# Changed places of weight splits, query products and a first up step in a two-layer encoder

## The chip, the cores and the metric

The program runs on one core of a Trainium2 chip. The metric is the device time of one launch in microseconds (us). The engines are TensorE (PE in the profile; its weight loads are PEld), VectorE (DVE), ScalarE (ACT), GpSimd (POOL) and SyncE (SP, which here only issues DMAs). "Granted clock" is the share of TensorE's full rate (2.4 GHz) that the trace records: 1.00 is the upper level, 0.50 the lower one (1.2 GHz).

## What is computed

A trunk of two layers on x of 1024 positions by 1024 channels, float32. Layer 0 mixes with an mLSTM, layer 1 with attention in a window of 128 positions to either side; both are followed by a SwiGLU with D_FF = 2816.

```python
def swiglu(h, w_in, w_out):
    gu = h @ w_in
    gate, up = gu[..., :D_FF], gu[..., D_FF:]
    return (jax.nn.silu(gate) * up) @ w_out

def window_attn_mixer(h, positions, w_in, sink, w_out):   # 16 query heads, 4 key heads, head 64, block L = 128
    proj = h @ w_in
    ...
    q = rope(q, positions).reshape(B, NB, L, Hkv, G, hd)
    k = rope(k, positions)
    ...                                                   # a block sees its own 128 keys and the 128 on either side
    scores = jnp.einsum('bcqhgd,bckhd->bchgqk', q, k_band) * (hd ** -0.5)
    scores = jnp.where(mask[None, :, None, None], scores, -jnp.inf)
    m = jnp.maximum(jnp.max(scores, axis=-1), sink_l)
    p = jnp.exp(scores - m[..., None])
    denom = jnp.sum(p, axis=-1) + jnp.exp(sink_l - m)
    out = jnp.einsum('bchgqk,bckhd->bcqhgd', p, v_band) / denom...
    return out.reshape(B, S, Hq * hd) @ w_out

def reference(...):
    for i in range(2):
        hn = rmsnorm(x, norm_mix_w[i])
        x = x + (mlstm_mixer if i == 0 else window_attn_mixer)(hn, ...)
        x = x + swiglu(rmsnorm(x, norm_ffn_w[i]), ffn_w_in[i], ffn_w_out[i])
    return rmsnorm(x, norm_final_w)
```

## The kernel before

x is held transposed, 8 rows of 128 channels by 1024 positions. A product of two float32 matrices is three products of parts: every operand is cut into a high part (ACT: L187 for weights, L200 or L204 for values) and what is left of it (POOL: L188 for weights; DVE: L201 or L205 for values), and the multiplications are high by high, high by low and low by high. wh and wl are the two parts of a weight tile, hh and hl those of a row of hidden values, raw and hraw what a DMA brought in. Weight tiles come by `ahead()`, which splits the next tile and starts the load of one further on; `w()` takes the tile that was split. Each engine works off its own list of instructions in the order in which the program issues them, and waits only for the operands and buffers of the next one. That order is the source's; where two kinds of work are mixed, `weave(main, fill)` spreads the pieces of the second list between those of the first.

The up half of a feed-forward (`ffn_up`, L535) has 22 steps f, one for each 128 hidden channels. It uses a scheme of seven half products for a two-by-two split of the weights and of the channels, with sums of weights and sums of channel rows as operands: `left()` makes the weight side of a step (wa, wb, wc, wd with a trailing h or l), and `self.forms` holds the channel side, four pairs of rows (f, f12, f23, f34). Each call of `seven` (L525) is one half product over the four pairs k, 12 matmuls of 512 columns at L530, into one PSUM bank; `pa`, `pe`, `pb`, `pc`, `pd` are the banks, and pa and pb take a second product on top. DVE, ACT and POOL then form silu(gate) times up (L551 to L584) with R, the reciprocal root of the norm, and the step's row goes to HBM (`hkeep`, L586). Between the products `more()` issues one item of `todo`, mostly the split of the next step's weights; in the last step it issues `hidden` (L589), which brings a row back and cuts it into hh and hl.

The down half (`ffn_down`) works in chunks of rows; the first chunk has six. Before it begins it issues the rest of the `hidden` calls, one `ahead()` for the first weight tile and `load_x`. For each d of eight output rows and each half of the positions it issues 18 matmuls at L616 and adds the bank to x (L643); in the first half of each d it calls `ahead()` for the weights of the next one, and behind each d `hidden` for a row of the next chunk.

The attention (`attn`, L1341) first computes keys and the queries of group 0 (`rope_in`), then the values (L476). Queries and keys with their rotation go to HBM (`bounce`, L1175) and come back in the shape that the scores need (`load_q` L1211, `load_k` L1219), which takes a round trip. Then a loop of 35 rounds i runs over 32 units (4 groups of heads by 8 blocks) in a pipeline: round i issues the scores and the softmax of unit i (`attn_soft`: matmul L1259, mask and maximum L1264 on DVE, exponential L1268 and L1269 on ACT, sums L1274 and L1275 on DVE, scaling L1276 on POOL), the transposes of unit i-2 (L1288) and the product with the values of unit i-3 (L1303, results to `ykeep` L1317 for groups 0 and 1). A unit of eight at position 6 of its group also issues the loads of the next group's queries and keys. Between these pieces stand the query products of groups 1 to 3: `qs` has 144 parts of two matmuls each (L228), twelve parts make one product, and four products one group, whose finished values go through `bounce`. They are spread evenly over the rounds 0 to 19:

```python
if i < NQ:                        # NQ = 20
    k = len(qs) * (i + 1) // NQ
    fill, nq = qs[nq:k], k
```

From round 20 on the output products of groups 0 and 1 (`outs`, also L228) fill the rounds; `take_back` (L699) brings the stored results of a group back from `ykeep` in round 19 and 20 and cuts them. Behind the loop `out_pair(self.y23, True)` adds the other two groups; behind every second row of it `norm_forms` makes the channel side of the next up half and squares the rows into the norm sum (R, L292; matmuls of the norm sum L364), and at its last quarter (`i == 3`) it issues `left()`, all weight sides of the first up step.

## Time and profile before

| | |
|---|---|
| time, median of 3 runs | 2365.91 us (2365.62 to 2366.03) |
| profiled execution, its own time | 2360.96 us |
| its span, first to last instruction | 2359.2 us |
| mean granted clock of TensorE | 0.978 |
| chain that ended last | PE 80%, DVE 6%, DMA 4%, issue 4%, POOL 3%, ACT 2% |
| three longest lines of that chain | L530 36% (up), L616 21% (down), L228 12% (dense and output products) |

The profiled execution is one of its own, 4.95 us below the median of the timed runs, and 1.76 us of it lie outside the span. All start times below count from the span's beginning. On this span layer 0's up half ends near 959 us, its down half near 1190; the attention's loop lies between 1300 and 1590, layer 1's up half between 1642 and 2085. A line of a timeline reads: start, duration, engine, line, operation, output <- inputs, shape, count, and in square brackets how long the engine had been idle before it and what released it.

### The profile page before, as it was taken

Reading aid. Unit: us, or ns where it says so; the run is one execution under the profiler, and the core shown is the slowest. Engines: PE = TensorE matmul, PEld = TensorE weight load, DVE = VectorE, ACT = ScalarE, POOL = GpSimd, SP = SyncE. Lnnn points to the kernel's source line nnn. Section 1 sums busy time; section 2 is a strip of 40 time slices with the busy share of each in tenths; the row PEclk is TensorE's granted clock in tenths of the full one; section 3 lists DMA queues with packets and bytes.
Section 4 is the critical chain, followed back from the end, with each engine's and each line's share of the span. In section 5 each row is a group of like instructions: output and inputs, shape, how many; then the busy total and the mean of one; then the engine's idle time right before and its main releaser. Section 6 shows DMA issues by size and latency. Waiting matters only on the chain.

```text
span 2359.2 us, 28227 instructions
## 1 busy us (share of the span) xinstructions
PE 2225.9 (94%) x10655; PEld 1827.1 (77%) x10655; DVE 1409.1 (60%) x2603; ACT 834.3 (35%) x1533; POOL 602.3 (26%) x410
## 2 busy tenths in 40 slices
PE   6999999989999999899998888798999999989998
PEld 3889988867888888688877766586788888868887
DVE  6455656688666666671233767778866666643113
ACT  3334445353222222221322666674322222232021
POOL 4212213311111111230432444550111111123043
PEclk9999999999999999999999999999999999999999
DMA  3111114132222222541315134602222222264112
GB/s 120 50 36 46 63 37 152 54 116 72 81 81 81 81 83 87 214 134 45 107 54 169 52 117 126 217 10 98 90 81 81 81 81 81 76 222 131 45 54 72
DMA packets 75960, 216.76 MB, mean 92 GB/s; under 512 B 8320, under 2 KB 14976, under 8 KB 75824
## 3 DMA queue, kind: packets, MB, share of 16 engines
q1 hardware_dynamic: 64216, 177.07, 23.1%
q10 hardware_dynamic: 11608, 37.89, 4.0%
q8 instruction: 84, 1.38, 0.2%
q14 instruction: 52, 0.43, 0.1%
HBM read 159.15 MB, written 55.77 MB: 91 GB/s over the span
## 4 chain that ended last, share of the span: by engine, by line
PE 80%; DVE 6%; DMA 4%; issue 4%; POOL 3%; ACT 2%; SPq 1%; POOLq 0%; ACTq 0%; DVEq 0%
PE mm L530 36%; PE mm L616 21%; PE mm L228 12%; PE mm L476 4%; PE pn L212 2%; DMA slab<-bounce 1%; DMA bounce<-slab 1%; PE sc L1259 1%; PE mx L1303 1%; PE tp L1288 1%; POOL wl L188 1%; PE pk L212 1%; DMA slab<-ykeep 1%; POOL e L1276 1%; DVE hnl L205 0%
## 5 line engine op out<-in xcount | busy, mean ns | idle before, releaser
L188 POOL TENSOR_TENSOR wl<-raw,wh 128x1024 fp32r<-128x1024 f32 (+2 forms) x96 | 231.0, 2410 | 593.2 <-ACT wh L187 372.2
L616 PE MATMUL mm<-hh,wh 128*128 128x512 f32 (+1 forms) x768 | 290.8, 379 | 13.1 <-ACT wh L187 13.1
L616 PE MATMUL mm<-hh,wl 128*128 128x512 f32 (+1 forms) x768 | 290.1, 378 | 3.1 <-POOL wl L188 3.1
L616 PE MATMUL mm<-hl,wh 128*128 128x512 f32 (+1 forms) x768 | 290.3, 378 | 0.0
L568 POOL TENSOR_TENSOR t<-t,R 128x512 f32<-128x512 f32 x44 | 57.5, 1308 | 618.1 <-ACT t L567 618.1
L616 PEld LDWEIGHTS mm<-hh,wh 128*128 128x128 f32 x768 | 145.6, 190 | 42.5 <-ACT wh L187 14.0
L643 DVE TENSOR_TENSOR x<-x,mm 128x512 f32<-128x512 f32 x80 | 54.9, 686 | 202.6 <-PE mm L616 202.6
L616 PEld LDWEIGHTS mm<-hh,wl 128*128 128x128 f32 x768 | 145.6, 190 | 33.0 <-POOL wl L188 4.5
L616 PEld LDWEIGHTS mm<-hl,wh 128*128 128x128 f32 x768 | 145.7, 190 | 28.6
L228 PE MATMUL mm<-slab,wh 128*128 128x512 f32 x512 | 153.0, 408 | 8.4 <-ACT wh L187 5.1
L567 ACT ACTIVATE t<-t 128x512 f32<-128x512 f32 x44 | 27.8, 632 | 329.0 <-DVE t L566 328.9
L530 PE MATMUL mm<-f12h,wbh 128*128 128x512 f32 x352 | 138.8, 395 | 0.4 <-ACT wbh L200 0.4
L530 PE MATMUL mm<-f12h,wbl 128*128 128x512 f32 x352 | 138.8, 394 | 0.0
L530 PE MATMUL mm<-f12l,wbh 128*128 128x512 f32 x352 | 138.6, 394 | 0.0
L187 ACT ACTIVATE wh<-raw 128x1024 fp32r<-128x1024 f32 (+3 forms) x106 | 102.0, 969 | 72.5 <-DVE hl L201 56.6
L228 PE MATMUL mm<-hnh,wh 128*128 128x512 f32 x416 | 126.4, 404 | 0.9 <-DVE x L643 0.9
L228 PE MATMUL mm<-hnh,wl 128*128 128x512 f32 x416 | 124.7, 400 | 0.0
L228 PE MATMUL mm<-hnl,wh 128*128 128x512 f32 x416 | 124.1, 399 | 0.0
L560 DVE TENSOR_TENSOR t<-mm,t 128x512 f32<-128x512 f32 x44 | 30.4, 692 | 154.3 <-PE mm L530 154.3
L228 PEld LDWEIGHTS mm<-slab,wh 128*128 128x128 f32 x512 | 96.4, 193 | 29.1 <-ACT wh L187 6.3
L1276 POOL TENSOR_TENSOR e<-e,smd 128x768 f32<-128x768 f32 (+1 forms) x64 | 87.4, 1369 | 121.9 <-DVE smd L1275 69.2
L530 PE MATMUL mm<-f34h,wd 128*128 128x512 f32 x352 | 117.1, 393 | 0.0
(296 smaller groups left out, 5320.5 us busy)
## 6 DMA issues: line engine op xcount, KB each, us to landing
raw<-in_ffn_in_dram SPq DMA_DIRECT2D x88, 512.0 KB
hkeep<-hs ACTq DMA_DIRECT2D x44, 512.0 KB
hraw<-hkeep SPq DMA_DIRECT2D x44, 512.0 KB
raw<-in_ffn_out_dram SPq DMA_DIRECT2D x32, 512.0 KB
raw<-in_m_in_dram SPq DMA_DIRECT2D x24, 512.0 KB
xkeep<-x ACTq DMA_DIRECT2D x24, 512.0 KB
x<-xkeep SPq DMA_DIRECT2D x48, 256.0 KB
bounce<-slab SPq DMA_DIRECT2D x40, 256.0 KB
```

The costliest lines, as they stand in the source:

```text
L187: nc.scalar.activation(hi[:, c], r[:, c], AF.Copy)
L188: (nc.vector if fast else nc.gpsimd).tensor_tensor(lo[:, c], r[:, c], hi[:, c].bitcast(F32), op=ALU.subtract)
L212: self.nc.tensor.matmul(out, lhsT=l, rhs=r, start=start and i == 0, stop=stop and i == len(jobs) - 1,)
L228: self.nc.tensor.matmul(st["ps"], lhsT=l, rhs=r, start=j == 0, stop=j == len(jobs) - 1)
L476: self.nc.tensor.matmul(st[c], lhsT=l, rhs=r, start=j == 0 and a == 0, stop=j == 1 and a == len(jobs) - 1)
L530: self.nc.tensor.matmul(ps, lhsT=l[a][:, c], rhs=r[b], start=start and k + a + b == 0, stop=stop and k == 3 and a == 1, skip_group_check=True,
L560: V.tensor_tensor(u2, pb, p1, op=ALU.add)
L567: A.activation(g0, g0, AF.Silu)
L568: G.tensor_tensor(g0, g0, R0, op=ALU.mult)
L616: nc.tensor.matmul(po, lhsT=l, rhs=r, start=j == 0, stop=j == len(jobs) - 1)
L643: V.tensor_tensor(x, x, po, op=ALU.add)
L1276: G.tensor_tensor(e[:, j:j + 2, :n], e[:, j:j + 2, :n], d.unsqueeze(2).broadcast_to([P, 2, n]), op=ALU.mult,)
```

## The change

Three places are changed.

First, at the border from the up to the down half (both layers): `ahead()`, the split of the first weight tile of the down half, becomes the first item of the last up step's `todo`, ahead of three `hidden` calls in place of four; the rest of `hidden` stays before `ffn_down`'s loop. The first `settle()` (it issues the sums of the norm, which were kept back) moves up by one product.

Second, at the start of an up half: in `out_pair` the weight sides of the first step are issued at i == 2 instead of 3, and the first up step computes pairs 0 to 2 of five half products (9 matmuls each) before pair 3 of any, into five banks at once; pair 3 follows at the places where the products stood. In `seven` the three multiplications of a pair stand in the order that `three` gives.

Third, in the attention: the first 24 parts of `qs` (two products) are issued before the loop. The others follow a table: all of group 1 by round 4, group 2 by round 11, group 3 by round 19. The results of group 0 are loaded back in round 13 and cut in 14, those of group 1 in rounds 20 and 21, and the output products begin in round 21.

```diff
@@ -522,15 +522,16 @@
 
         return out, [one, two_, three_, four]
 
-    def seven(self, out, ps, left, right, start=True, stop=True):
-        for k, f in enumerate(self.forms):
+    def seven(self, out, ps, left, right, start=True, stop=True, ks=range(4)):
+        jobs = []
+        for k in ks:
             c = slice(k * P, (k + 1) * P)
-            l, r = out[left], f[right]
-            for a, b in ((0, 0), (0, 1), (1, 0)):
-                self.nc.tensor.matmul(
-                    ps, lhsT=l[a][:, c], rhs=r[b], start=start and k + a + b == 0,
-                    stop=stop and k == 3 and a == 1, skip_group_check=True,
-                )
+            l, r = out[left], self.forms[k][right]
+            jobs += three([((l[0][:, c], l[1][:, c]), r)])
+        for j, (l, r) in enumerate(jobs):
+            self.nc.tensor.matmul(
+                ps, lhsT=l, rhs=r, start=start and j == 0, stop=stop and j == len(jobs) - 1, skip_group_check=True,
+            )
 
     def ffn_up(self, i):
         nc = self.nc
@@ -541,25 +542,35 @@
             if f + 1 < NF:
                 nxt, todo = self.left()
             else:
-                nxt, todo = None, [lambda k=k: self.hidden(i, k) for k in range(FF_CHUNKS[0][1] - 2)]
+                nxt, todo = None, [self.ahead] + [lambda k=k: self.hidden(i, k) for k in range(3)]
             more = lambda: todo.pop(0)() if todo else None
             hs = self.unit(name="hs")
             R0, R1 = self.Rv(0), self.Rv(1)
-            pa = self.bank("mm")
-            self.seven(cur, pa, "a11", "b11")
+
+            rest = dict(start=False, ks=range(3, 4)) if f == 0 else {}
+            if f == 0:
+                pa, pe, pb, pc, pd = (self.bank("mm") for _ in range(5))
+                for ps, l, r in ((pa, "a11", "b11"), (pe, "s4", "b22"), (pb, "s2", "t2"), (pc, "s1", "t1"), (pd, "a22", "t4")):
+                    self.seven(cur, ps, l, r, stop=False, ks=range(3))
+            else:
+                pa = self.bank("mm")
+            self.seven(cur, pa, "a11", "b11", **rest)
             p1 = self.t2()
             A.activation(p1, pa, AF.Copy)
-            pe = self.bank("mm")
-            self.seven(cur, pe, "s4", "b22")
+            if f:
+                pe = self.bank("mm")
+            self.seven(cur, pe, "s4", "b22", **rest)
+            self.settle()
             more()
             self.seven(cur, pa, "a12", "b21", start=False)
-            pb = self.bank("mm")
-            self.seven(cur, pb, "s2", "t2")
-            self.settle()
+            if f:
+                pb = self.bank("mm")
+            self.seven(cur, pb, "s2", "t2", **rest)
             u2 = self.t2()
             V.tensor_tensor(u2, pb, p1, op=ALU.add)
-            pc = self.bank("mm")
-            self.seven(cur, pc, "s1", "t1")
+            if f:
+                pc = self.bank("mm")
+            self.seven(cur, pc, "s1", "t1", **rest)
             self.settle()
             V.tensor_tensor(u2, pc, u2, op=ALU.add)
             g0 = self.t2()
@@ -578,8 +589,9 @@
             V.tensor_tensor(c22, pc, u3, op=ALU.add)
             V.tensor_tensor(hs[:, HALF:], u2, c22, op=ALU.mult)
             more()
-            pd = self.bank("mm")
-            self.seven(cur, pd, "a22", "t4")
+            if f:
+                pd = self.bank("mm")
+            self.seven(cur, pd, "a22", "t4", **rest)
             V.tensor_tensor(u3, pd, u3, op=ALU.add)
             V.tensor_tensor(hs[:, :HALF], g0, u3, op=ALU.mult)
             more()
@@ -680,7 +692,7 @@
                 nc.vector.tensor_tensor(x, x, po, op=ALU.add)
                 if last and e % 2 and half:
                     i = e // 2
-                    if i == 3:
+                    if i == 2:
                         self.first, todo = self.left()
                         for f in todo:
                             f()
@@ -1363,8 +1375,13 @@
             qs = sum((self.rope_in(1 + g, -0.125) for g in range(1, 4)), [])
             y01 = [[], []]
             outs = self.out_pair(y01)
-            nq = no = 0
-            backs = []
+            nq = len(qs) // 6
+            for f in qs[:nq]:
+                f()
+
+            plan = ((0, nq), (4, len(qs) // 3), (11, 2 * len(qs) // 3), (19, len(qs)), (n + 3, len(qs)))
+            no = 0
+            backs = {}
             for i in range(n + 3):
                 so, sc = self.attn_soft(*units[i], st[i]) if i < n else ([], [])
                 tr = self.attn_tr(*units[i - 2], st[i - 2]) if 2 <= i <= n + 1 else []
@@ -1374,19 +1391,19 @@
                 if i % NC == 6 and i < n - NC:
                     g = i // NC + 1
                     main[-1] += [lambda: self.load_q(g), lambda: self.load_k(g)]
-                if i in (NQ - 1, NQ):
-                    j = i + 1 - NQ
-                    backs.append(self.take_back(self.ykeep[3 + j], y01[j]))
+                for j in range(2):
+                    if i == (13, NQ)[j]:
+                        backs[j] = self.take_back(self.ykeep[3 + j], y01[j])
+                    if i == (14, NQ + 1)[j]:
+                        backs[j]()
                 if i == NQ:
-                    for f in backs:
-                        f()
                     self.load_x(self.xkeep)
-                if i < NQ:
-                    k = len(qs) * (i + 1) // NQ
-                    fill, nq = qs[nq:k], k
-                else:
-                    k = max(0, len(outs) * (i - NQ) // (n + 2 - NQ))
-                    fill, no = outs[no:k], k
+                (i0, n0), (i1, n1) = [(p, q) for p, q in zip(plan, plan[1:]) if p[0] <= i < q[0]][0]
+                k = n0 + (n1 - n0) * (i + 1 - i0) // (i1 - i0)
+                fill, nq = qs[nq:k], k
+                if i > NQ:
+                    k = len(outs) * (i - NQ) // (n + 2 - NQ)
+                    fill, no = fill + outs[no:k], k
                 weave([lambda m=m: [f() for f in m] for m in main], fill)
             self.norm_begin(3, "forms")
             weave(self.out_pair(self.y23, True))
```

ACT at layer 0's border from up to down, before; t is a value of the step, hkeep the store of its row, raw_7927 and raw_7929 the first two weight tiles of the down half:

```order
L200 ACTIVATE hh_8149<-hraw_8147 128x1024
L567 ACTIVATE t_1398_8139<-t_1398_8139 128x512
L571 ACTIVATE t_1396_8123<-t_1396_8123 128x512
L586 DMA hkeep_21_90<-hs_8063 128x1024
L200 ACTIVATE hh_8172<-hraw_8170 128x1024
L200 ACTIVATE hh_8193<-hraw_8191 128x1024
L200 ACTIVATE hh_8200<-hraw_8198 128x1024
L200 ACTIVATE hh_8206<-hraw_8204 128x1024
L187 ACTIVATE wh_8212<-raw_7927 128x768
L187 ACTIVATE wh_8261<-raw_7929 128x768
```

and now:

```order
L187 ACTIVATE wh_8094<-raw_7927 128x768
L559 ACTIVATE t_1390_8077<-mm_8064 128x512
L598 DMA hkeep_20_89<-hs_7933 128x1024
L200 ACTIVATE hh_8149<-hraw_8147 128x1024
L578 ACTIVATE t_1398_8139<-t_1398_8139 128x512
L582 ACTIVATE t_1396_8123<-t_1396_8123 128x512
L598 DMA hkeep_21_90<-hs_8063 128x1024
L200 ACTIVATE hh_8172<-hraw_8170 128x1024
L200 ACTIVATE hh_8193<-hraw_8191 128x1024
L200 ACTIVATE hh_8200<-hraw_8198 128x1024
L200 ACTIVATE hh_8206<-hraw_8204 128x1024
L200 ACTIVATE hh_8212<-hraw_8210 128x1024
```

The first weight split moved from behind all the hh to the step before the store of the last row; five hh stand behind that store where four stood, and the second weight tile follows them.

SP at the end of group 1's queries, before (the slabs with bounce are the rotated queries of group 1, slab<-bounce the start of `load_q` for units 8 to 15):

```order
L1317 DMA ykeep_66<-R_9210 256x1x128
L1175 DMA bounce_118<-slab_10941 4x32x512
L1175 DMA bounce_118<-slab_10942 4x32x512
L1175 DMA bounce_118<-slab_10941 4x32x512
L1175 DMA bounce_118<-slab_10942 4x32x512
L1317 DMA ykeep_66<-R_9210 256x1x128
L1211 DMA slab_10963<-bounce_118 128x1024
```

and now:

```order
L1187 DMA bounce_118<-slab_10734 4x32x512 x2
L1187 DMA bounce_118<-slab_10735 4x32x512 x2
L1329 DMA ykeep_66<-R_9210 256x1x128 x2
L168 DMA raw_10917<-in_a_in_dram 128x1024
L1223 DMA slab_11010<-bounce_118 128x1024
L1329 DMA ykeep_66<-R_9210 256x1x128
```

Two stores of results and one weight load now stand between the last store of the queries and the load that reads them, where one store of results stood; and a store of results follows the load's first DMA.

PE at the start of the loop, before (the last value products, then unit 0's scores and the first query product):

```order
L1259 MATMUL sc_10404<-slab_10239,slab_10176 128x256
L1259 MATMUL sc_10404<-slab_10240,slab_10176 128x256
L228 MATMUL mm_10416<-hnh_9244,wh_10412 128x512
L228 MATMUL mm_10416<-hnh_9311,wh_10412 128x512
```

and now, the end of the second query product and unit 0's scores:

```order
L228 MATMUL mm_10441<-hnh_9666,wl_10403 128x512
L228 MATMUL mm_10441<-hnh_9737,wh_10402 128x512
L228 MATMUL mm_10441<-hnl_9738,wh_10402 128x512
L228 MATMUL mm_10441<-hnh_9737,wl_10403 128x512
L1271 MATMUL sc_10474<-slab_10239,slab_10176 128x256
L1271 MATMUL sc_10474<-slab_10240,slab_10176 128x256
L228 MATMUL mm_10480<-hnh_9244,wh_10437 128x512
```

48 matmuls of the query products moved from between the scores to ahead of the first of them.

## Rows read from the trace of the kernel before

**Rows 1.** Busy time of each engine over the whole span:
```profile
PE 2225.9 (94%) x10655; PEld 1827.1 (77%) x10655; DVE 1409.1 (60%) x2603; ACT 834.3 (35%) x1533; POOL 602.3 (26%) x410
```

**Rows 2.** Windows: start:end us, PE, PEld, DVE, ACT, POOL, PEclk, DMA share, GB/s
```profile
1300.00:1305.00 5.00, 4.53 (x15) 3.74 (x16) 1.74 (x7) 2.12 (x8) 0.00 (x0) 0.59 0.11 43
1305.00:1370.00 65.00, 61.11 (x324) 50.96 (x323) 53.29 (x141) 46.05 (x126) 32.93 (x23) 1.00 0.23 75
1370.00:1381.00 11.00, 4.93 (x17) 3.85 (x16) 2.19 (x6) 2.06 (x7) 1.77 (x1) 0.76 0.80 219
1381.00:1435.00 54.00, 48.41 (x251) 38.99 (x250) 44.59 (x131) 40.78 (x118) 28.52 (x20) 0.99 0.26 84
1435.00:1447.00 12.00, 5.27 (x19) 4.50 (x18) 2.67 (x7) 2.76 (x7) 3.38 (x2) 0.59 0.78 227
1447.00:1476.00 29.00, 26.26 (x138) 21.52 (x137) 25.86 (x71) 21.52 (x63) 15.64 (x12) 0.99 0.27 85
1476.00:1500.00 24.00, 14.97 (x56) 11.14 (x56) 17.01 (x34) 13.52 (x34) 13.64 (x11) 0.79 0.67 228
1540.00:1590.00 50.00, 49.84 (x267) 41.46 (x266) 40.21 (x110) 38.93 (x105) 28.79 (x22) 1.00 0.04 12
```

**Rows 3.** Waits of PE in the loop: total us, times, longest us
```profile
PE sc L1259 <- DMA slab<-bounce: 12.8, 2, 6.7
PE sc L1259 <- DMA raw<-in_a_in_dram: 11.2, 1, 11.2
```

**Rows 4.** Chain that ended last, attention: start us, us, work
```profile
1588.67 22.76 PE mm L228 x98
```

**Rows 5.** Timeline of PE, first products of layer 0's down half
```profile
965.16 0.79 PE L616 MATMUL mm<-hh,wh 128*128 128x512 f32 x1 [6.54 <-ACT wh L187]
967.91 0.79 PE L616 MATMUL mm<-hh,wl 128*128 128x512 f32 x1 [1.53 <-POOL wl L188]
```

**Rows 6.** Timeline of ACT and DVE, the same place
```profile
960.48 3.90 ACT L200 ACTIVATE hh<-hraw 128x1024 fp32r<-128x1024 f32 x4 [4.54 <-DVE hs L584]
961.57 4.63 DVE L201 TENSOR_TENSOR hl<-hraw,hh 128x1024 fp32r<-128x1024 f32 x4 [1.49 <-ACT hh L200]
```

**Rows 7.** Timeline of ACT, DVE and POOL, weights of d = 2, layer 0
```profile
977.47 1.06 ACT L200 ACTIVATE hh<-hraw 128x1024 fp32r<-128x1024 f32 x1 [11.63 <-DMA hraw<-hkeep]
978.43 0.69 DVE L643 TENSOR_TENSOR x<-x,mm 128x512 f32<-128x512 f32 x1 [3.50 <-PE mm L616]
979.34 2.64 POOL L188 TENSOR_TENSOR wl<-raw,wh 128x768 fp32r<-128x768 f32 x1 [9.70 <-ACT wh L187]
```

**Rows 8.** Timeline of DVE and POOL, the same in layer 1
```profile
2104.74 0.69 DVE L643 TENSOR_TENSOR x<-x,mm 128x512 f32<-128x512 f32 x1 [3.50 <-PE mm L616]
2106.01 2.27 POOL L188 TENSOR_TENSOR wl<-raw,wh 128x768 fp32r<-128x768 f32 x1 [10.14 <-ACT wh L187]
```

**Rows 9.** Timeline of PE and DVE, first up step of layer 1
```profile
1641.81 0.70 PE L530 MATMUL mm<-f,wah 128*128 128x512 f32 x2 [0.97 <-DVE x L680]
1660.26 1.22 DVE L292 TENSOR_TENSOR R<-R,sq 128x1024 f32<-128x1024 f32 x1
1663.18 1.84 PE L364 MATMUL mx<-ones,R 128*128 128x1 f32 x16
1679.62 0.80 PE L530 MATMUL mm<-f23h,wah 128*128 128x512 f32 x1 [3.63 <-ACT t L551]
```

**Rows 10.** Timeline of PE, unit 0
```profile
1300.41 1.16 PE L1259 MATMUL sc<-slab,slab 128*128 128x256 f32 x2 [11.20 <-DMA raw<-in_a_in_dram]
```

**Rows 11.** Timeline of SP and PE, load of unit 8's queries and its use
```profile
1364.64 1.77 SPq L1211 DMA_DIRECT2D slab<-bounce  x4
1376.55 0.76 PE L1259 MATMUL sc<-slab,slab 128*128 128x256 f32 x2 [6.07 <-DMA slab<-bounce]
```

**Rows 12.** Lines, loop: DVE's sums; then two of them in the timeline
```profile
L1274 DVE TENSOR_TENSOR smd<-smd,sme 128x2 f32<-128x2 f32 x64 | 26.5, 414 | 9.1 <-ACT sme L1269 8.8
1324.05 0.16 DVE L1274 TENSOR_TENSOR smd<-smd,sme 128x2 f32<-128x2 f32 x1
1342.35 1.67 DVE L1274 TENSOR_TENSOR smd<-smd,sme 128x2 f32<-128x2 f32 x1 [0.37 <-ACT sme L1269]
```

## The prediction

> **What bounds the kernel now.** I read the engines' totals first. PE is busy for 94% of the span and no other engine for over 60% [rows 1], so a change can pay in two ways only: it takes idle time of PE away, or time in which PE works at its lower clock. Then I looked for both near the three places of the change. In the attention's loop the windows show them side by side [rows 2]: in 1305 to 1370 PE is busy 61.11 of 65 us at a clock of 1.00, but in 1370 to 1381, 1435 to 1447 and 1476 to 1500 only 4.93 of 11, 5.27 of 12 and 14.97 of 24 us, at 0.76, 0.59 and 0.79. The list of waits says what the first two of these are: the scores wait twice for queries that come back from HBM, 12.8 us in all, and once 11.2 us at the loop's start [rows 3]. Last I read the timelines of the two borders, where PE stands 6.54 and 1.53 us for the first weights of the down half [rows 5] and 0.97 us for x ahead of the up half [rows 9]. One matmul of 512 columns takes 22.76 / 98 = 0.232 us where nothing holds PE [rows 4].
>
> In the undisturbed 148 us of the loop (1305 to 1370, 1381 to 1435, 1447 to 1476) PE idles 3.9 + 5.6 + 2.7 = 12.2 us and DVE is busy 53.29 + 44.59 + 25.86 = 123.7 us, 84% [rows 2]. That is the second thing to see: with PE's long waits gone DVE stands close behind it. Eight units take from 1300.41 to the beginning of the wait at 1376.55 - 6.07 = 1370.48 [rows 10, 11], 8.76 us each, and DVE works 8.76 x 53.29 / 65 = 7.2 us of a unit, PE about 8.2.
>
> **First change, the border from up to down, twice.** Nothing is added or removed; the split of the first weights (wh on ACT, wl on POOL) goes ahead of the last step's own values, one hh behind the store goes after. Both waits go, since wh and wl are then ready before the up half ends at about 958.6 (965.16 - 6.54) [rows 5]. What is late next is the hidden values: hh comes every 3.90 / 4 = 0.97 us, hl every 4.63 / 4 = 1.16 us [rows 6], five of each behind the store instead of four; the six products of one row (two halves by three) take PE 1.39 us, so PE keeps roughly to their pace and ends d = 0 between 969 and 972, where it ended at 978.43 [rows 7]. That would be 6.4 to 9.4 us. But d = 2 needs its own weights, and these come no earlier: ACT stands until 977.47 for hraw, then makes wh, and POOL's wl ends at 979.34 + 2.64 = 981.98 [rows 7]. That ACT wait is on a transfer which the change doesn't move. From there PE has at least 32 of the 36 matmuls of d = 2 left, so it ends at 982.0 + 32 x 0.232 = 989.4, at most 990.9 with a late start; before, it ended at 978.43 + 72 x 0.232 = 995.1. So 4.2 to 5.7 us. Layer 1 has the same shape: wl of d = 2 ends at 2106.01 + 2.27 = 2108.28, d = 0 ended at 2104.74 [rows 8], and the same count gives the same gain. I take 5 each, **-10** together; the ends are -3 each (five hh in front of the second weight tile make d = 1 wait) and -9 each (hraw comes earlier too).
>
> **Second change, the first up step, twice.** The weight sides are made a quarter earlier, so PE can begin on three pairs of rows while the last one is made. But nothing of the sum to which the step leads moves: the norm's last row is squared and added by DVE until 1660.26 + 1.22 = 1661.5, PE adds it up at 1663.18 and waits at 1679.62 for the gate's value, 3.63 us [rows 9]. DVE makes the same instructions in another order. The start of PE gets later, if anything (the last x of layer 1 now stands behind weight splits on DVE), and the wait of 3.63 us covers that, as PE's work of some 30 us before it still fits. I take **-0.5** for both; the ends are -3 (each gate 1.5 us earlier) and +2.
>
> **Third change, the attention.** Two of twelve query products, 48 matmuls or 48 x 0.232 = 11.1 us, go ahead of the loop, into a wait of 11.20 us for the load of the first queries and keys [rows 10]. PE thus arrives at 1300.2 with the load just there, and with no idle time before it. They issue two DVE operations each, no store yet, and one weight load, which stands behind the load of the queries and keys on SP. The terms:
>
> - The clock at the start. In 1300 to 1305 it was 0.59 [rows 2], 5 x 0.41 = 2.0 us lost after the wait. PE no longer stops there: -2.0.
> - The two waits for queries, 12.8 us [rows 3], and the lower clock behind them: of 4.93 and 5.27 us of PE work in these windows some 4.5 and 5.2 lie behind the wait at the lower level [rows 2, 11], half of which is lost: 2.2 and 2.6. Now the last store of a group's queries lies two units before its load, where it lay directly before it, so the load no longer waits for the stores. -17.5 in all.
> - In their place comes a wait of the load for SP. Most of its DMAs now stand behind the store of a unit's results, which is ready two units (17.5 us) before the queries are used; from issue to use it takes 1376.55 - 1364.64 = 11.9 us [rows 11], and the issues ahead of it some 3 us. That fits by 2 to 3 us, without much to spare; a wait of 0 to 4 us at each of two places: +4.
> - The take-backs. 1476 to 1500 holds 24 - 14.97 = 9.0 us of idle time [rows 2], where both groups' results come back, are cut and x is loaded at once. One of the two is now done in rounds 13 and 14, the other still lies at 20 and 21: -4, between 0 and -9.
> - The 11.1 us of PE work that leave the loop. If PE sets the pace they are all gained; if DVE does, only its share goes, four operations of about 0.6 us, 2.4 us. PE idles 8% there with DVE at 84% busy, which is nearer to the second, so -4.
>
> Sum -2.0 - 17.5 + 4 - 4 - 4 = **-23.5**.
>
> DVE's sums show how it and POOL get in each other's way: L1274 on two columns takes 0.16 us alone and 1.67 us while POOL cuts a weight tile, 0.414 us in the mean of 64 [rows 12]. The Trainium skill ("SBUF — State Buffer", "Who interferes with whom") says that a DVE instruction with two inputs in SBUF contends with a GpSimd instruction that reads SBUF, and that whoever comes first holds the port for its whole instruction; the trace agrees, with the 1.67 us. By this rule a loop that runs closer together has more such meetings: if their share doubled, 64 x (0.414 - 0.16) = 16 us would come onto DVE, and the time of the first rival below would go from 2342 to 2358; by the rows alone nothing is added. The sum above goes without it.
>
> **The sum.** -10 - 0.5 - 23.5 = -34.0 against the profiled execution, 2360.96 - 34.0 = 2327.0. The median of the timed runs lies 4.95 us above that execution, so 2331.9, **2332 us**.
>
> **Rivals.**
>
> 1. DVE paces the loop. For it: 84% busy, 7.2 of 8.76 us of each unit, and the rounds until 4 hold as many query parts as before. Then of the load waits half remain, since the stores that feed them come as late as DVE lets them (-8.75), the take-backs give nothing, the products moved 2.4: with the clock of the start -13.2, in all -23.7, so 2342. Against it: at 1540 to 1590 PE is busy 49.84 of 50 us while DVE does 40.21 [rows 2], so a pipeline with DVE at 80% can keep PE full.
> 2. PE paces it all. The whole 11.1 us, the 9.0 us of the take-backs, both waits and no new one: -39.6, in all -50.1, so 2316. The same row 1540 to 1590 speaks for it; the 12.2 us of idle time in the undisturbed stretches against it.
> 3. The attention's change doesn't do what it says: the stores of a group are no longer the last thing, but the load behind them is as late, for the reason of the SP row above, and what is won before is lost there. Only the borders pay: -10.5, 2355. Against it speak the two units of distance.
> 4. Slower than before: the granted clock. Rounds 0 to 3 and 11 to 18 now hold 6 parts instead of 7.2, so PE has 8.2 - 1.2 x 0.46 = 7.6 us of work where DVE needs 7.2 us, and short waits in each of these 12 rounds, 91 us of PE work. If that brought the lower level for half of it, 46 us would be lost, 2378. It decides from 34 + 5 = 39 us of such work on. For it: after each long wait the clock stands at 0.5 to 0.6 [rows 2]. Against it: in 1305 to 1370 and in 1447 to 1476 it stayed at 1.00 and 0.99 with 6 and 9% of idle time.
>
> **How the numbers follow.** Forecast 55% (its own range 2322 to 2344, from the ends of the new wait, the take-backs and the first change), rival 1 20%, rival 2 13%, rival 3 8%, rival 4 4%. The range is 2316 to 2354: it takes in the forecast, rival 1 and most of rival 2, and leaves out half of rival 2, rival 3's upper part and rival 4, some 15%. A measurement of this kernel tells 0.2%, 4.7 us, from no change. Faster by more than that are the forecast, rivals 1 and 2 and a quarter of rival 3: 90%; the rest of rival 3, where the borders give less than 5 us together, is 6%; slower is rival 4, 4%.
>
> **What would show it.** In the profile after: no PE wait for wh or wl at the start of either down half, and a POOL wl of d = 2 that ends within 1 us of where it did relative to the hraw transfer, with a PE wait in front of d = 2; the norm sums and the gate of both first up steps at the same distance from the last x; no PE wait ahead of unit 0 and a clock near 1.00 behind it; the waits for slab<-bounce at 0 to 8 us instead of 12.8; the idle time around the take-backs at about 5 us in round 20. The prediction is wrong if the load waits come back at units 8, 16 or 24, if the loop's rounds take longer than 8.8 us each with DVE above 90% busy, or if the clock in rounds 11 to 18 falls below 0.9.

## The result, and the profile after

The changed kernel takes 2332.49 us (median of 4 runs, 2330.67 to 2334.53), the kernel before, run beside it, 2365.76 us (4 runs, 2358.82 to 2366.03). The ratio is 0.9867, 95% interval 0.9847 to 0.9886, or 31 us less (27 to 36). Forecast were 2332 us, and 2316 to 2354.

The page after, busy time of each engine, shows PE's share up from 94% [rows 1] to 96% of a shorter span:

```profile
PE 2228.1 (96%) x10655; PEld 1826.9 (78%) x10655; DVE 1421.6 (61%) x2603; ACT 832.8 (36%) x1533; POOL 608.7 (26%) x410
```

The attention's loop in windows after (columns as in [rows 2]); the units lie elsewhere now, so the windows are cut at other times:

```profile
1305.00:1310.00 5.00, 4.62 (x24) 3.61 (x23) 3.14 (x10) 2.37 (x10) 0.00 (x0) 1.00 0.11 45
1310.00:1368.00 58.00, 52.12 (x269) 42.61 (x268) 51.52 (x131) 41.58 (x118) 32.38 (x22) 0.97 0.42 123
1368.00:1432.00 64.00, 58.05 (x306) 47.00 (x305) 56.69 (x150) 48.96 (x137) 35.83 (x24) 1.00 0.44 130
1432.00:1458.00 26.00, 19.55 (x98) 14.39 (x96) 24.12 (x57) 17.69 (x50) 16.17 (x11) 1.00 0.26 80
1458.00:1482.00 24.00, 19.77 (x82) 14.77 (x83) 19.18 (x52) 17.47 (x52) 11.80 (x10) 0.86 0.82 288
1517.00:1567.00 50.00, 49.14 (x265) 41.23 (x263) 41.01 (x111) 38.69 (x104) 28.91 (x22) 1.00 0.04 11
```

Unit 0 begins at 1305.48 with no wait over 0.25 us and at a clock of 1.00 (0.59 before). Of the waits of 6.1 and 6.7 us at units 8 and 16, 0.5 us is left at unit 8, but in 1368 to 1432 DVE is busy for 89% and in 1432 to 1458 for 93%, and there PE idles 6 and 6.5 us. The waits of PE in the loop after say the same (columns as in [rows 3]): the loads, 12.8 and 11.2 us before, are down to 0.8, and what is left is mostly DVE.

```profile
PE mx L1315 <- DVE R L1322: 6.7, 5, 4.5
PE sc L1271 <- DVE smm L1276: 5.5, 6, 2.6
PE tp L1300 <- DVE t L201: 5.2, 10, 1.6
...
PE sc L1271 <- DMA slab<-bounce: 0.8, 2, 0.5
```

At the borders from up to down, PE after no longer waits 6.54 us for wh [rows 5]. It runs on into the down half, waits some 1.6 us for hh behind its first matmuls, and later for wl or wh of d = 2; first layer 0, with POOL's wl, then layer 1:

```profile
968.15 0.73 PE L628 MATMUL mm<-hh,wh 128*128 128x512 f32 x2 [1.57 <-ACT hh L200]
987.80 0.50 PE L628 MATMUL mm<-hh,wl 128*128 128x512 f32 x1 [0.83 <-POOL wl L188]
985.61 2.14 POOL L188 TENSOR_TENSOR wl<-raw,wh 128x768 fp32r<-128x768 f32 x1 [10.01 <-ACT wh L187]
2066.48 0.73 PE L628 MATMUL mm<-hh,wh 128*128 128x512 f32 x2 [1.59 <-ACT hh L200]
2083.73 0.50 PE L628 MATMUL mm<-hh,wh 128*128 128x512 f32 x1 [0.86 <-ACT wh L187]
2085.95 0.50 PE L628 MATMUL mm<-hh,wl 128*128 128x512 f32 x1 [1.50 <-POOL wl L188]
```

And in the first up step of layer 1 (DVE's last x and norm rows, then PE; compare [rows 9]) PE waits 5.40 us at the start where it waited 0.97, because that x stands behind weight splits and channel sums on DVE:

```profile
1622.23 0.68 DVE L692 TENSOR_TENSOR x<-x,mm 128x512 f32<-128x512 f32 x1
1636.25 2.55 DVE L292 TENSOR_TENSOR R<-R,sq 128x1024 f32<-128x1024 f32 x2
1623.05 1.19 PE L532 MATMUL mm<-f,wah 128*128 128x512 f32 x2 [5.40 <-DVE x L692]
1640.50 1.84 PE L364 MATMUL mx<-ones,R 128*128 128x1 f32 x16
1657.47 0.79 PE L532 MATMUL mm<-f23h,wah 128*128 128x512 f32 x1 [3.41 <-ACT t L559]
```

But before, PE stopped twice more within its first ten matmuls, which it no longer does; with the 0.97 us these waits came to 4.7 us:

```profile
1643.99 0.50 PE L530 MATMUL mm<-f,wal 128*128 128x512 f32 x1 [1.48 <-DVE wal L201]
1648.14 0.50 PE L530 MATMUL mm<-f23h,wch 128*128 128x512 f32 x1 [2.26 <-ACT wch L200]
```

To see where the time went I cut both traces at the same instructions, always from start to start. "First step" runs from the fifth-last addition to x ahead of the up half (the 28th of 32) to the 241st matmul of the up half; "border" from the last matmul of the up half to the 1001st of the down half; a unit begins with its first mask. The table gives the length before and the difference from it, in us, for the profiled execution of the changed kernel and of six experiments below; a star marks a stage whose instructions are those of before, so the starred numbers show how much one stage moves from one kernel's profile to the next with nothing changed in it: up to 1.8 us. Ahead of the first row, where no kernel differs, the profiles lie up to 4.1 us apart (that addition starts between 502.4 and 506.5 us over all runs, 502.8 before, 506.5 in the changed kernel).

| stage | before | all three | first | second | third | first + third | products ahead | table alone |
|---|---|---|---|---|---|---|---|---|
| layer 0 first step | 82.6 | +2.9 | +1.8* | +2.9 | +0.7* | +0.8* | 0.0* | +0.8* |
| layer 0 border | 243.6 | -1.5 | -1.4 | +0.5* | -0.2* | -2.7 | 0.0* | -0.2* |
| units 0 to 7 | 77.2 | -15.6 | +1.8* | +0.2* | -16.1 | -15.2 | -14.5 | -7.0 |
| units 8 to 15 | 67.0 | -2.6 | 0.0* | -1.3* | -1.5 | -2.0 | -5.5 | -5.9 |
| units 16 to 23 | 78.6 | -10.3 | -0.4* | +0.5* | -10.3 | -8.7 | -0.9 | -3.0 |
| layer 1 first step | 84.4 | +2.2 | 0.0* | 0.0 | -0.5* | -1.6* | +0.5* | -1.5* |
| layer 1 border | 231.0 | -4.4 | -3.6 | -0.9* | -0.9* | -4.8 | +0.3* | +0.1* |

### The profile page after: what moved, and what is told of

It reads as the page before. It is cut to its first block, busy times and chain, and to the rows that moved or that the text cites. A ratio compares the mean times of both kernels' runs of the same rounds, so it can differ in the third digit from the quotient of the medians.

```text
span 2332.8 us, 28234 instructions
## 1 busy us (share of the span) xinstructions
PE 2228.1 (96%) x10655; PEld 1826.9 (78%) x10655; DVE 1421.6 (61%) x2603; ACT 832.8 (36%) x1533; POOL 608.7 (26%) x410
## 4 chain that ended last, share of the span: by engine, by line
PE 77%; DVE 8%; issue 5%; DMA 4%; POOL 2%; ACT 2%; SPq 1%; POOLq 0%; ACTq 0%; DVEq 0%
PE mm L532 37%; PE mm L628 18%; PE mm L228 12%; PE mm L476 4%; PE pn L212 2%; DMA raw<-in_a_in_dram 1%; PE sc L1271 1%; POOL wl L188 1%; DVE smd L1286 1%; PE pk L212 1%; DMA slab<-bounce 1%; PE tp L1300 1%; PE mx L1315 1%; ACT e L1280 1%; DVE e L1276 1%
## 5 line engine op out<-in xcount | busy, mean ns | idle before, releaser
L188 POOL TENSOR_TENSOR wl<-raw,wh 128x1024 fp32r<-128x1024 f32 (+2 forms) x96 | 233.7, 2439 | 594.0 <-ACT wh L187 391.2
L228 PE MATMUL mm<-slab,wh 128*128 128x512 f32 x512 | 152.8, 407 | 6.1 <-ACT wh L187 3.1
L228 PE MATMUL mm<-hnh,wh 128*128 128x512 f32 x416 | 124.6, 399 | 0.9 <-DVE x L655 0.9
L228 PE MATMUL mm<-hnl,wh 128*128 128x512 f32 x416 | 124.5, 401 | 0.0
L228 PE MATMUL mm<-hnh,wl 128*128 128x512 f32 x416 | 124.1, 398 | 0.0
L532 PE MATMUL mm<-f,wah 128*128 128x512 f32 x352 | 113.0, 403 | 10.8 <-DVE x L692 10.8
L228 PEld LDWEIGHTS mm<-slab,wh 128*128 128x128 f32 x512 | 95.9, 193 | 26.8 <-ACT wh L187 4.1
```

The lines of the kernel that those rows point to most:

```text
L188: (nc.vector if fast else nc.gpsimd).tensor_tensor(lo[:, c], r[:, c], hi[:, c].bitcast(F32), op=ALU.subtract)
L228: self.nc.tensor.matmul(st["ps"], lhsT=l, rhs=r, start=j == 0, stop=j == len(jobs) - 1)
L532: self.nc.tensor.matmul(ps, lhsT=l, rhs=r, start=start and j == 0, stop=stop and j == len(jobs) - 1, skip_group_check=True,)
```

## The experiments

**One change at a time.** Each of the three alone, then the first and third together. The edits are the parts of the diff above that go with these lines, in this order: `todo` of the last up step; `i == 2` with `seven` and the rest of `ffn_up`; `attn`. The earlier `settle()`, told above under the first change, thus ran with the second; it moves up by two half products, not one.

```diff
-                nxt, todo = None, [lambda k=k: self.hidden(i, k) for k in range(FF_CHUNKS[0][1] - 2)]
+                nxt, todo = None, [self.ahead] + [lambda k=k: self.hidden(i, k) for k in range(3)]
...
-                    if i == 3:
+                    if i == 2:
...
-            nq = no = 0
-            backs = []
+            nq = len(qs) // 6
```

> The first change alone (first weight split of the down half moved ahead, both layers). Theory A, from the two profiles: the early start wins 6 to 7 us at each border, but layer 0 gives 4.7 us back at the next chunk of rows, where DVE is full with the rotation tables, so 1.4 + 4.9 = 6.3 us faster, 2359.5, and a PE wait for wl near the second chunk of layer 0 that layer 1 doesn't have. Rival B, the prediction's term: 5 us at each border and no loss later, 2355.8. If the layer 0 loss in the profile came from the later start of layer 0's up half and not from DVE's extra work, it is absent here and B holds.

Measured: 2359.26 us (11 runs), ratio 0.998 (0.9972 to 0.9989), 2.6 to 6.6 us faster. The stages have -1.4 and -3.6; theory A holds in kind, B's 10 us lie outside the interval. PE waits 2.3 us for wl near the second chunk of layer 0, as A said.

> The second change alone (weight sides a quarter earlier, three pairs of rows first). Theory A, from the two profiles: the last x stands behind more DVE work, PE starts 4.5 us later, the norm's sum and the gate come 1 to 2 us later and PE stays longer at its lower clock behind the gate: 2.4 to 3.3 us slower in each layer, 5.4 us in all, 2371.2. Rival B, the prediction's term: the wait for the gate covers the later start, 0.5 us faster, 2365.3. What the profile of this run should show under A is a gate of layer 1's first step that lies more than 1 us later behind the last output product than in the kernel before.

Measured: 2363.83 us (12 runs), ratio 1.0005 (0.9996 to 1.0014), between 0.9 us faster and 3.3 us slower. A's 5.4 us are outside, B's -0.5 inside. Layer 1's first step is as long as before, and its gate lies 0.7 us later behind the last output product, where A named more than 1; so the 2.2 us that the changed kernel's profile shows in layer 1 are not the rule. Layer 0's first step is 2.9 us longer. That isn't shown to be the change's cost either: in the kernels here without the second change (the last run apart) the same stage is 0 to 2.2 us longer than before, and in the run below with all three and two additions, 0.9.

> The third change alone (query products and stored outputs of the attention). Theory A, from the two profiles: 28.5 us faster, 2337.3, with 28 us less from unit 0 to unit 31. Rival B, the prediction's sum of terms: 23.5 us faster, 2342.3, the rest of the difference between the profiles being chance of the single execution.

Measured: 2333.03 us (4 runs), ratio 0.9874 (0.986 to 0.9887), 27 to 33 us faster; the three stages of the loop sum to -27.9. A holds, B's 23.5 is too little.

> The first and the third change without the second. Theory A: the second change costs 5.4 us, so this beats the changed kernel, 2365.8 - 6.3 - 28.5 = 2331.0 by the profiles' ledger, or 5.4 us below the changed kernel's 2332.5, 2327. Rival B, the second change gives 0.5 us: 2333.0, not below the changed kernel.

Measured: 2329.87 us (4 runs), ratio 0.9861 (0.9846 to 0.9876). It lies 2.6 us below the changed kernel's median, but the two intervals overlap: not decided here.

**What takes layer 0's border back.** In the changed kernel PE stands before the second chunk for wl, whose wh waited on ACT for an hl of DVE:

```profile
1040.51 0.50 PE L628 MATMUL mm<-hh,wl 128*128 128x512 f32 x1 [2.31 <-POOL wl L188]
1036.35 1.06 ACT L187 ACTIVATE wh<-raw 128x1024 fp32r<-128x1024 f32 x1 [2.43 <-DVE hl L201]
```

The next run thins the rotation tables (`side`) that DVE makes there:

```diff
-                    for _ in range(3):
+                    for _ in range((2, 3)[ci]):
                         next(side, None)
```

> First and third change, and in the first chunk of layer 0's down half two steps of the rotation tables behind each d instead of three (three in the second chunk, as before). Theory A: DVE, busy all the time there, makes wh and wl of the second chunk late (wh waits for hl), and takes back 4.6 us of what layer 0's border had won. Then with a third less of that work the PE waits of 0.3 and 2.3 us for wh and wl near the second chunk go and 3 to 4.6 us come back: 2326 against 2329.9 of the two changes alone. Rival B: the late thing is a transfer (hraw or raw) that cannot come earlier; then the wait stays, 2329.9. Rival C: the tables get late at the other end and cost more in the second chunk, over 2332.

Measured: 2325.76 us (4 runs), ratio 0.9851 (0.9834 to 0.9867). The border of layer 0 is 5.0 us shorter than before, where it was 2.7 with the two changes alone and 1.5 with all three. The windows of the changed kernel and then of this run (columns as in [rows 2]) show the hole in the first and none in the second:

```profile
1016.00:1032.00 16.00, 16.00 (x71) 12.95 (x70) 15.86 (x15) 1.91 (x2) 2.45 (x1) 1.00 0.27 96
1032.00:1044.00 12.00, 9.38 (x36) 6.99 (x35) 11.86 (x11) 4.01 (x4) 6.13 (x2) 0.92 0.34 119
```

```profile
1016.00:1032.00 16.00, 16.00 (x70) 12.95 (x69) 15.83 (x15) 3.64 (x4) 3.48 (x1) 1.00 0.46 161
1032.00:1044.00 12.00, 11.85 (x51) 9.31 (x50) 11.93 (x9) 4.52 (x5) 8.64 (x3) 1.00 0.27 91
```

DVE is full in both, but in the second what PE needs comes in time. Theory A is shown for the stage: over all kernels with the first change, layer 0's border is 1.4 to 2.7 us shorter than before in the four with three table steps and 3.8 to 5.0 in the four with two, 2.4 us between the means, which is less than the 3 to 4.6 that A named. The kernel before has no wait over 0.25 us at the second chunk. For the whole time the two intervals overlap.

**The third change in parts.** First the two products ahead of the loop alone, then the table of rounds alone.

```diff
+            nq = n0 = len(qs) // 6
+            for f in qs[:nq]:
+                f()
...
-                    k = len(qs) * (i + 1) // NQ
+                    k = n0 + (len(qs) - n0) * (i + 1) // NQ
```

```diff
+            plan = ((0, 0), (4, len(qs) // 3), (11, 2 * len(qs) // 3), (19, len(qs)), (NQ, len(qs)))
...
-                    k = len(qs) * (i + 1) // NQ
+                    (i0, n0), (i1, n1) = [(p, q) for p, q in zip(plan, plan[1:]) if p[0] <= i < q[0]][0]
+                    k = n0 + (n1 - n0) * (i + 1 - i0) // (i1 - i0)
```

> Of the third change only the two query products ahead of the loop; the other 120 parts evenly over rounds 0 to 19, stored results as before. Evenly spread, group 1 is then done in round 3 and group 2 in round 11, nearly as in the table of the change. Theory A: this is what moves the loads ahead of their use, so the waits for slab<-bounce (12.8 us) go and all of the gain up to round 20 is here: 18 to 20 us faster, 2344 to 2346, and only the take-backs' 8 to 10 us are missing. Rival B: the table of rounds is what does it; then at least one of the two waits stays and the gain is 8 us (11.1 us of products and 2.0 us of clock, part of it lost to DVE), 2355.

Measured: 2341.65 us (4 runs), ratio 0.9916 (0.99 to 0.9932), 16 to 24 us faster. Theory A: the load waits are gone with the products alone, and the wait for R (L1310) that [rows 3] did not have is there. Two rows of its waits in the loop:

```profile
PE mx L1303 <- DVE R L1310: 10.1, 5, 4.4
...
PE sc L1259 <- DMA slab<-bounce: 0.2, 1, 0.2
```

> Of the third change only the table of rounds (all of group 1 by round 4, group 2 by round 11, group 3 by round 19), nothing ahead of the loop, stored results as before; so rounds 0 to 3 hold twelve parts each. Theory A: the loads come early and the two waits of 12.8 us and the lower clock behind them go, but the wait of 11.2 us before unit 0 stays and the eleven us of products stay in the loop: 10 to 15 us faster, 2349 to 2354. Rival B: DVE paces the loop, what PE no longer waits for at units 8 and 16 it waits for elsewhere; less than 5 us faster, above 2358.6.

Measured: 2346.85 us (4 runs), ratio 0.9939 (0.9922 to 0.9956), 10 to 18 us faster, as A has it. One wait for a load is left, and it is the one before unit 0; all others together are 0.9 us. So either part alone brings the loads ahead of their use:

```profile
PE sc L1259 <- DMA slab<-bounce: 12.2, 2, 11.3
```

**What paces the loop now.** The changed kernel's L1286 (L1274 before) takes longer than before [rows 12]:

```profile
L1286 DVE TENSOR_TENSOR smd<-smd,sme 128x2 f32<-128x2 f32 x64 | 34.8, 544 | 6.6 <-ACT sme L1281 6.6
```

0.544 us in the mean instead of 0.414; 11 of the 64 take over 1 us, 7 did before. In both traces every one of these sums that takes over 0.3 us (20 before, 30 after) begins while a TENSOR_TENSOR runs on POOL and ends within 0.04 us behind it, and no shorter one lies wholly inside such an operation; the longest of the changed kernel, with POOL's:

```profile
1497.34 2.29 DVE L1286 TENSOR_TENSOR smd<-smd,sme 128x2 f32<-128x2 f32 x1 [0.71 <-ACT sme L1281]
1497.20 2.41 POOL L188 TENSOR_TENSOR wl<-raw,wh 128x1024 fp32r<-128x1024 f32 x1 [1.86 <-ACT wh L187]
```

The edit gives the sum a scalar per partition in place of the second tensor:

```diff
-            V.tensor_tensor(d, d, ek[:, j:j + 2], op=ALU.add)
+            for c in range(j, j + 2):
+                V.tensor_scalar(dn[:, c:c + 1], dn[:, c:c + 1], ek[:, c:c + 1], None, op0=ALU.add)
```

> First and third change, and the two-column sum of the softmax on DVE (0.41 us in the mean, 1.2 to 1.7 us beside POOL) as two operations of one column whose second operand is a scalar per partition, not a second input tensor. Theory A: the long ones are a meeting of two inputs in SBUF with POOL's reads; without a second input tensor they take 0.1 to 0.2 us each, DVE gains some 5 to 10 us in the loop and, as DVE is busy for 89 to 93% in rounds 8 to 20, PE gets 2 to 6 us of it: 2324 to 2328. Rival B: the length has another cause (the wait for ACT's value, counted into the operation), the mean of the pair stays at 0.3 to 0.4 us and the time at 2329.9.

Measured: 2318.09 us (5 runs), ratio 0.9812 (0.9796 to 0.9829), some 11 us below the two changes alone (0.9861), more than A forecast. Its line:

```profile
L1275 DVE TENSOR_SCALAR smd<-smd,sme 128x1 f32<-128x1 f32 x128 | 24.8, 207 | 5.8 <-ACT sme L1269 4.9
```

Twice as many operations take 10.0 us less, and the longest of the 128 takes 0.22 us, though 50 of them lie wholly inside an operation of POOL, as here:

```profile
1378.90 0.21 DVE L1275 TENSOR_SCALAR smd<-smd,sme 128x1 f32<-128x1 f32 x1
1378.80 2.43 POOL L188 TENSOR_TENSOR wl<-raw,wh 128x1024 fp32r<-128x1024 f32 x1
```

With that, rival B falls: a pair does take 0.39 us, but the long ones are gone and the time is not 2329.9. The Trainium skill ("SBUF — State Buffer", "Who interferes with whom") says that a DVE instruction with two inputs in SBUF contends with a GpSimd instruction that reads SBUF, and that one with at most one such input, outside the 2-port perf modes, does not. Both traces agree, with 2.29 and 0.21 us beside L188 of POOL; in which mode the operations on one column ran, they don't tell.

The gain lies in the loop, but not evenly: units 16 to 23, where 5 of the 11 long sums were, are 10.9 us shorter than with the two changes alone, units 0 to 15 only 2.5, and the last units 2.2 longer. Why the freed time of DVE turns into PE's time mostly there was not tested.

**Both additions, with and without the second change, and POOL in the first step.**

```diff
-            self.split(*wb, s12)
+            self.split(*wb, s12, eng)                      # in the POOL run alone; eng is GpSimd, for wd too
```

> First and third change, the softmax sums by column and two table steps behind each d, together. Theory A: the two gains lie at different places and add, 11.8 + 4.1 us below the 2329.9 of the two changes alone: 2314. Rival B: the earlier loop meets the next limit (transfers, ACT) and only part adds, 2317 or more.

Measured: 2320.02 us (5 runs), ratio 0.9816 (0.9803 to 0.9829): no gain over the sums alone. The stage of layer 0's border has its 3.8 us, but this profile's first step of layer 0 is 2.2 us longer than before with the same instructions. In the loop a load is late again, as B has it: PE waits 1.9 us for slab<-bounce at unit 24, where no such wait was over 0.3 us with the sums alone. Whether the gains add is left open.

> The changed kernel with all three changes, and the same two additions; it differs from the run beside it only by the second change, which is thus measured on the same chip. Theory A, from the stages of the second change run alone: about 2 us slower in layer 0 and 0 to 2 us in layer 1, 2316 to 2318 where the other is 2314. Rival B, the prediction's term: 0.5 us faster, not slower than the run beside it.

Measured: 2317.53 us (4 runs, 2315.54 to 2318.56), ratio 0.9803 (0.9789 to 0.9816), the lowest median here, 2.5 us below the run beside it, though the intervals overlap. With that, A falls: the second change is not a loss of 2 us or more in every company. With the second change alone at a ratio of 1.0005, and the first and third without it 2.6 us below all three, its sign stays open; by its own run it lies between 0.9 us faster and 3.3 us slower.

> As the two changes with both additions; besides, the low parts wbl and wd of the first up step are made on POOL, which stands idle there for 34 us, instead of DVE, which is full until the norm's sum. Theory A, two inputs in SBUF: POOL's subtractions read SBUF and hold up DVE's operations with two inputs in the same stretch, so little or nothing comes of the 1.8 us that leave DVE in each layer: within 1 us of the run beside it, and single DVE operations of 0.7 us stretched to 1.5 us and more. Rival B, no such meeting: the norm's sum and the gate come 1.8 us earlier in each layer, 3.6 us in all, 2310.

Measured: 2322.72 us (4 runs, 2318.68 to 2327.39), ratio 0.9826 (0.981 to 0.9843): 2.7 us above the run beside it by the medians, where A said within 1, and not the 2310 of B; the intervals overlap. What two inputs cost is plain in its timeline, POOL first, then DVE:

```profile
1612.32 2.51 POOL L201 TENSOR_TENSOR wbl<-s,wbh 128x1024 fp32r<-128x1024 f32 x1 [19.02 <-ACT wbh L200]
1614.79 1.73 POOL L201 TENSOR_TENSOR wd<-raw,wd 128x512 fp32r<-128x512 f32 x1
1612.46 2.91 DVE L508 TENSOR_TENSOR s<-raw,s 128x512 f32<-128x512 f32 x1
1615.30 1.77 DVE L205 SCALAR_TENSOR_TENSOR f<-x,nw,f 128x512 fp32r<-128x512 f32 x1
```

L508 takes 0.68 us elsewhere and 2.91 here, f 0.75 and 1.77: of the 1.8 us that left DVE more than 3 came back.

## Why the prediction was right

The time came out half a microsecond beside the forecast, and that is partly luck: the first change, measured alone by the medians, gave 4.3 us where 10 were forecast, the third 30.6 where 23.5 were, and the two errors nearly cancel. None of the prediction's three signs of being wrong came: no load wait over 0.5 us in the loop, 7.7 to 8.6 us a unit up to unit 23, and the clock at 1.00 in rounds 11 to 18. Its sums hold; one reading does not, said under the rivals.

**First change, forecast -10.** Measured -2.6 to -6.6; the step that failed is "5 each", in layer 0. The gain up to d = 2 is there in both layers, bounded by the weights of d = 2 as written: counted from the end of the up half, wl of d = 2 ends at 22.4 to 23.5 us in every kernel here, and d = 3, which began at 36.3 us before, begins at 30.1 in layer 0 of the changed kernel and at 32.0 in layer 1 (36.4 before). What the step left out is what DVE does behind it: in layer 0 it also makes the rotation tables, had no room for PE to come earlier, and took most of it back at the next chunk. The thinned tables show it. Layer 1, without that work, has -3.1 to -5.3 over the eight kernels with the first change, about the 4.2 to 5.7 of the count.

**Second change, forecast -0.5 with ends at -3 and +2.** Alone between -0.9 and +3.3. The later start (PE waits 5.40 us) was foreseen. In layer 1 it is covered, but hardly by the wait for the gate, as the prediction had it: that wait shrinks only from 3.63 to 3.41 us. Two earlier stops, of 1.48 and 2.26 us, go. In layer 0 it stays open: with the change alone PE's norm sum begins 1.6 us later behind the fifth-last x than before, but up to 1.8 later in kernels that don't have the change.

**Third change, forecast -23.5, measured -27 to -33, -27.9 in its stages.** The terms, from the two parts; they are differences of single profiles that add up to -27.9 by construction, each with the 1 to 2 us of the starred stages:

- The clock at the start, -2.0: from unit 0 to unit 1 it was 5.50 us, and is 3.72 in the changed kernel, -1.8. Of these some 0.7 are not the clock: 11 matmuls of L228 lie between the two masks where 14 did.
- The two waits with their clock, -17.5: the table alone, which leaves unit 0's wait and the products where they were, gives -7.0 - 5.9 - 3.0 = -15.9 in the loop.
- The products ahead, -4: the two products alone give -14.5 - 5.5 - 0.9 = -20.9; if the waits are worth the same 15.9 there and unit 0 the 1.8, that leaves -3.2. PE did not gain the 11.1 us; DVE, at 87 to 89% in units 0 to 23, stands in the way, as the sums by column bear out.
- The new wait for SP, +4: 0.8 us in the waits after, which the parts above already hold. This is the term that was most over-sized; the load of unit 8 still lands 0.5 us after PE asks for it, so the margin is as thin as was worked out.
- The take-backs, -4: all three parts give -27.9 and the products alone -20.9, so -7, the table's share included. It is -9.4 in units 16 to 23 and +4.0 in units 8 to 15, where group 0's results now come back, a cost that the term didn't have. The place is right, the size is nearer the upper end of 9.

**Rivals.** Rival 1 (DVE) is half true: DVE is at 89 to 93% from 1368 to 1458 and most of PE's remaining waits are on it, and less work on it then gave 11 us; but it did not keep the load waits, which went whole. Its reason that the rounds until 4 hold as many query parts as before is misread: they hold 24, where they held 28. Rival 2 fails on the same rows. Rival 3 falls with the third change alone. Rival 4 falls: the clock is 0.97 from 1310 to 1368, which holds most of the thinner rounds 0 to 3, and 1.00 from 1368 to 1458, with rounds 11 to 18.

The meetings of DVE's sums with POOL were weighed in the prediction with 16 us more on DVE if they doubled. The long sums grew by about half, 7 to 11 over 1 us, and L1286 took 8.3 us more, without carrying the time to rival 1's.

## What to carry to other kernels

When a wait goes, look at which engine stands next in busy share at that place, and at what else it does there a chunk later: the first change's gain was lost some 70 us behind the place where it was won, to work that had nothing to do with it. Work that fits in a hole that is there anyway (two products in the 11.2 us before unit 0) can pay twice, once for itself and once because all that follows it in order comes earlier; by the count above the second was the larger part. Short operations of two tensors beside another engine's reads can cost ten times their length; their mean, not their best, goes into the sum.

## What had not been expected

A sum over two columns, 64 times in the kernel, held 11 us of the whole time, more than the first and second change together: 34.8 us of DVE at 0.544 us each against 0.16 for one alone [rows 12]. And a stage of 80 us with the very same instructions varies by up to 2.2 us from one kernel's profile to the next, so terms under 2 us can't be read from one profile each.
